# Second layer of a two-layer decoder trunk: residual and block-sum loads queued behind the last pair's T blocks, and the receptance split queued behind the copies of T's lower products

## The chip, the cores and the metric

The kernel runs on one core of one Trainium2 chip. The metric is device time in microseconds (us), lower is better. The engines are named as the profile names them: PE is TensorE's matmul path and PEld its weight loads, DVE is VectorE, ACT is ScalarE, POOL is GpSimd, SP is SyncE, which issues most DMAs here. A letter q behind an engine's name (SPq) means its sequencer, which issues DMAs in order.

## The reference, cut to what matters

`x` has 512 tokens of 2048 channels, all in float32. Layer 0 is gated differential attention, layer 1 is gated RWKV-7 time mixing; each adds its output to `x`. The change lies in layer 1 alone:

```
hn = rms_norm(x);  p = hn @ w_in;  p = p + (shift(p) - p) * mu
r, k, v, g, dw, da = split(p)
decay = exp(-exp(-softplus(-(w0 + tanh(dw) @ decay_up)) - 0.5));  a = sigmoid(a0 + da @ iclr_up)
kk = normalise(k * k_k);  k = k * (1 + (a - 1) * k_a)
per head (32 heads of 64), over the 512 tokens:
    S = S * w_t + (S a_t) b_t^T + v_t k_t^T ;   y_t = S r_t         (a = -kk, b = kk * a)
y = group_norm(y) + sum(r * k * r_k) * v;   x = x + (y * silu(g)) @ w_out
```

## The kernel before

Every large product is made of three passes in a fast float32 format: an operand is split into a high part (rounded by ACT) and a low part (the rest, by DVE), and `mm3` adds high*high, high*low and low*high. The activations of the current layer lie split in `g.hH` and `g.hL`; weights come from memory in 512 KB pieces (`wraw`, three buffers), and `split_w` splits them (`wh` by ACT at L105, `wl` by DVE at L106).

Layer 1 walks over 16 pairs of heads (`for j in range(D // P)` in `layer1`). For a pair it projects k, r, v and the gate with 48 matmuls each (`proj`). The recurrence is done in 8 chunks of 64 tokens. For each chunk a triangular system must be inverted; its inverse is called T. The steps of T that the change and the prediction touch:

- `gram` makes the products `gp` of keys and queries (PE, L1317), copies them to `G` (ACT, L1324) and stores parts of them, with the key norms `ssl` (ACT, L1304), to a scratch `ltd` in memory.
- `t_solve` loads them as `LT` and solves all 32-wide diagonal blocks at once on DVE (`tmpl`, `Tm`, L1376 to L1385); the result goes by DMA to a scratch `td` (L1386).
- `t_combine` loads the blocks from `td` into `TT` by four DMAs (L1405), transposes them on DVE (`T1`, L1415, one instruction for each of the two heads), multiplies on PE (`px<-T,G`, L1421), copies the product to `X` on ACT (L1424), and multiplies again (`px<-TT,X`, L1432) for T's lower block.
- `scan_pair` then goes through the 8 chunks with small matmuls `sm`; it begins with a memset of the first state `VS`.

These steps of one pair, a generator in a `Chain`, are taken in between the next pairs' projections, a step after a given number of matmuls (`tick`). A scheduler with priorities (`high_priority`) then orders each engine's instructions. `with tc.issue_after(ins)` adds one thing to this: what is traced inside it, as far as it is on the engine of `ins`, stands behind `ins` in that engine's order. It adds no wait between engines.

After the 16 pairs comes the output projection: the rows `yd2` are loaded and split (`split_rows`, L461 the loads `yr`), the first two column blocks of `w_out` are multiplied in the plain way (`unit_tok`, for `cb` 0 and 1), and the last two in a scheme with seven products (`seven`), which needs sums of blocks of the rows: `sum_forms` loads the rows again as `frow` (POOL's queue, L677). The old `x` is loaded as `xr` (SP's queue, L1725, 256 KB each, four for each `cb`) and added. All of these loads can be placed by the scheduler as early as their buffers are free: the two `xr` tiles of `cb` 1 take the buffers of `AR` of the pairs 13 and 14.

Beside T, each pair's receptance `r`, shifted and weighted (`mixr`, DVE, L1291), is split by `split_act` (`sHx` on ACT, L1112, `sLx` on DVE), for a sum over channels that `stage_v` takes later.

## Time and profile before

| | |
|---|---|
| time, median of 3 runs | 2075.96 us (2073.53 to 2079.5) |
| the profiled execution's own time | 2081.64 us |
| its span from first to last instruction | 2079.9 us |
| mean granted TensorE clock | 0.997 |
| PE busy | 2055.6 us |
| DVE busy | 1605.1 us |
| ACT busy | 1124.4 us |
| POOL busy | 383.2 us |

The profiled execution took 5.7 us longer than the median of the plain runs, and 1.7 us of its time lie outside the span. Times of rows are us from the span's start. In a row of the timeline stand: start, duration, engine, line, operation, output<-inputs, count, and in brackets the idle time of the engine before it with what ended it. In a row of a table by stages stand: the stage, its length, then for PE, PEld, DVE, ACT and POOL the busy time and the number of instructions, then the granted TensorE clock, the busy share of the 16 DMA engines, and GB/s.

### The profile page before, as it was taken

Reading aid. Unit: us, or ns where it says so; the run is one execution under the profiler, and the core shown is the slowest. Engines: PE = TensorE matmul, PEld = TensorE weight load, DVE = VectorE, ACT = ScalarE, POOL = GpSimd, SP = SyncE. Lnnn points to the kernel's source line nnn. Section 1 sums busy time; section 2 is a strip of 40 time slices with the busy share of each in tenths; the row PEclk is TensorE's granted clock in tenths of the full one; section 3 lists DMA queues with packets and bytes.
Section 4 is the critical chain, followed back from the end, with each engine's and each line's share of the span. In section 5 each row is a group of like instructions: output and inputs, shape, how many; then the busy total and the mean of one; then the engine's idle time right before and its main releaser. Section 6 shows DMA issues by size and latency. Waiting matters only on the chain.

```text
span 2079.9 us, 34162 instructions
## 1 busy us (share of the span) xinstructions
PE 2055.6 (99%) x11948; PEld 1680.2 (81%) x11948; DVE 1605.1 (77%) x4113; ACT 1124.4 (54%) x2238; POOL 383.2 (18%) x765
## 2 busy tenths in 40 slices
PE   9999999999999999999999999999999999999999
PEld 7888888888888888878777778888888888877887
DVE  6988988888888976475778888787777887866645
ACT  5765656565666544345555555555555555545322
POOL 1021211102111000101122322222222222231001
PEclk9999999999999999999999999999999999999999
DMA  8487978879787966823333323323333333345565
GB/s 271 135 178 195 174 176 186 162 196 162 190 176 170 271 214 175 175 80 107 101 82 87 96 77 104 87 86 95 106 92 98 90 95 91 107 136 172 186 163 121
DMA packets 158653, 294.61 MB, mean 142 GB/s; under 512 B 64416, under 2 KB 81824, under 8 KB 158480
## 3 DMA queue, kind: packets, MB, share of 16 engines
q1 hardware_dynamic: 110912, 184.91, 28.8%
q0 software_dynamic: 24928, 87.21, 22.6%
q10 hardware_dynamic: 22640, 20.30, 3.0%
q8 instruction: 94, 1.54, 0.3%
q14 instruction: 79, 0.65, 0.1%
HBM read 268.71 MB, written 23.66 MB: 141 GB/s over the span
## 4 chain that ended last, share of the span: by engine, by line
PE 81%; DVE 11%; DMA 4%; ACT 2%; issue 2%; ACTq 0%; SPq 0%; DVEq 0%; POOLq 0%
PE pp L122 40%; PE pp L573 22%; PE pt L122 5%; DVE wl L106 3%; PE sc L122 1%; PE sm L1509 1%; PE o L122 1%; DMA TT<-td 1%; DMA td<-Tm 1%; PE sm L1527 1%; DVE tmpl L1376 1%; PE gp L1317 1%; PE sm L1520 1%; PE lora L122 1%; PE z L122 1%
## 5 line engine op out<-in xcount | busy, mean ns | idle before, releaser
L106 DVE TENSOR_TENSOR wl<-wraw,wh 128x1024 fp32r<-128x1024 f32 (+2 forms) x291 | 356.1, 1224 | 194.2 <-ACT wh L105 187.7
L105 ACT CAST wh<-wraw 128x1024 fp32r<-128x1024 f32 (+2 forms) x291 | 303.7, 1044 | 269.8 <-PE pp L122 145.4
L122 PE MATMUL pp<-hL,wh 128*128 128x512 f32 x1024 | 414.9, 405 | 0.0
L122 PE MATMUL pp<-hH,wl 128*128 128x512 f32 x1024 | 413.8, 404 | 0.0
L122 PE MATMUL pp<-hH,wh 128*128 128x512 f32 x1024 | 413.6, 404 | 0.0
L122 PEld LDWEIGHTS pp<-hH,wh 128*128 128x128 f32 x1024 | 193.6, 189 | 34.8 <-issue 0.4
L122 PEld LDWEIGHTS pp<-hL,wh 128*128 128x128 f32 x1024 | 193.5, 189 | 33.8
L122 PEld LDWEIGHTS pp<-hH,wl 128*128 128x128 f32 x1024 | 193.7, 189 | 32.4
L573 PE MATMUL pp<-wh,hH 128*128 128x512 f32 x448 | 176.8, 395 | 0.0
L573 PE MATMUL pp<-wh,hL 128*128 128x512 f32 x448 | 175.7, 392 | 0.0
L122 PE MATMUL pp<-wh,hH 128*128 128x512 f32 x372 | 146.5, 395 | 2.0 <-ACT hH L1103 1.8
L122 PE MATMUL pp<-wl,hH 128*128 128x512 f32 x372 | 146.8, 395 | 0.6 <-DVE wl L106 0.5
L122 PE MATMUL pp<-wh,hL 128*128 128x512 f32 x372 | 146.8, 395 | 0.1
L1376 DVE SCALAR_TENSOR_TENSOR tmpl<-LT,Tm 128x60 f32<-128x60 f32 (+24 forms) x496 | 134.2, 270 | 13.3
L573 PE MATMUL pp<-wl,hH 128*128 128x512 f32 x448 | 140.4, 392 | 0.0
L1515 POOL COPY SA<-VS 64x64 f32<-64x64 f32 x224 | 56.7, 253 | 418.3 <-DVE VS L1531 378.2
L1378 DVE TENSOR_TENSOR Tm<-Tm,tmpl 128x60 f32<-128x60 f32 (+24 forms) x496 | 104.1, 210 | 11.7
L1512 ACT COPY rhs<-sm 64x64 f32<-64x64 f32 x256 | 52.8, 206 | 91.2 <-PE sm L1509 88.6
L573 PEld LDWEIGHTS pp<-wl,hH 128*128 128x128 f32 x448 | 84.4, 188 | 17.2
L573 PEld LDWEIGHTS pp<-wh,hH 128*128 128x128 f32 x448 | 84.2, 188 | 17.3 <-issue 0.3
L573 PEld LDWEIGHTS pp<-wh,hL 128*128 128x128 f32 x448 | 84.2, 188 | 16.2
L1522 ACT COPY VS<-sm 64x64 f32<-64x64 f32 x256 | 52.7, 206 | 70.5 <-PE sm L1520 63.9
(402 smaller groups left out, 4376.6 us busy)
## 6 DMA issues: line engine op xcount, KB each, us to landing
wraw<-in_rw_w_in_dram SPq DMA_DIRECT2D x128, 512.0 KB
wraw<-in_da_w_in_dram SPq DMA_DIRECT2D x75, 512.0 KB
wraw<-in_da_w_in_dram POOLq DMA_DIRECT2D x28, 512.0 KB, 6.7
wraw<-in_da_w_out_dram SPq DMA_DIRECT2D x26, 512.0 KB
wraw<-in_rw_w_out_dram SPq DMA_DIRECT2D x26, 512.0 KB
Ta<-in_da_w_in_dram POOLq DMA_DIRECT2D x21, 512.0 KB, 5.7
Tb<-in_da_w_in_dram POOLq DMA_DIRECT2D x21, 512.0 KB, 5.7
Tc<-in_da_w_in_dram POOLq DMA_DIRECT2D x21, 512.0 KB, 5.5
```

Source lines behind the costliest of these rows:

```text
L105: a = nc.scalar.copy(hi[:, ks], raw[:, ks])
L106: d = nc.vector.tensor_sub(lo[:, ks], raw[:, ks], hi[:, ks].bitcast(F32))
L122: m = nc.tensor.matmul(out, a, b, start=s, stop=e, skip_group_check=skip)
L573: m = nc.tensor.matmul(out[t][:], x, wt[lo][:, k, :], start=first, stop=end and lo == 1 and k == KG - 1, skip_group_check=True)
L1317: m = nc.tensor.matmul(gp[h][:, i * P : (i + 1) * P], BK[r_, c0 + i, :, :], p.AR[r_, c0 + i, :, :], start=True, stop=True)
L1376: nc.vector.scalar_tensor_tensor(tt, LT[:, i : i + 1, i + 1 :].to_broadcast([P, s, n]), n2[:, i : i + 1], Tm[:, 0:s, i : i + 1].to_broadca ...
L1378: nc.vector.tensor_add(Tm[:, 0:s, i + 1 :], Tm[:, 0:s, i + 1 :], tt)
L1509: nc.tensor.matmul(sm[:, 0:P], both(p.G[:, c, 0]), both(VS[:, c]), start=True, stop=True)
L1512: nc.scalar.copy(rhs[r_, :], sm[r_, h * C : h * C + C])
L1515: nc.gpsimd.tensor_copy(p.SA[r_, c - 1, :], VS[r_, c, h, :])
L1520: nc.tensor.matmul(sm[:, P : P + C], both(g.TT[j % 2][:, c]), rhs[:], start=True, stop=True)
L1522: g.copied = nc.scalar.copy(VS[r_, c, h, :], sm[r_, P : P + C])
```

## The change

There are three edits, all of the same kind; no instruction is added or taken away.

1. `sum_forms`: the `frow` loads on POOL's queue stand behind the last traced memset of `VS` (`g.begun`).
2. The `xr` loads on SP's queue stand behind the last traced load of T's blocks, `TT<-td` (`g.blocks`). When they are traced, this is that of pair 15, the last one.
3. In the pairs for which `normed` holds, the split of the receptance stands, on ACT, behind the two copies of the product `px` to `X` (`g.lower`).

```diff
@@ sum_forms
-            nc.gpsimd.dma_start(out=r, in_=src[k0 * P : (k0 + KG) * P, :].rearrange(...))
+            with g.tc.issue_after(g.begun):
+                nc.gpsimd.dma_start(out=r, in_=src[k0 * P : (k0 + KG) * P, :].rearrange(...))
@@ t_combine
-            nc.sync.dma_start(
+            g.blocks = nc.sync.dma_start(
                 out=TT[h * C + o : h * C + o + HALF, :, h, o : o + HALF],
-                in_=g.td[j % 2].rearrange(...)[:, l0 : l0 + NC_, :])
+                in_=g.td[j % 2].rearrange(...)[:, l0 : l0 + NC_, :]).ins
...
-        nc.scalar.copy(X[hi], px[hi, :N].rearrange("p (c s) -> p c s", c=NC_))
+        g.lower = nc.scalar.copy(X[hi], px[hi, :N].rearrange("p (c s) -> p c s", c=NC_)).ins
@@ scan_pair
-        nc.gpsimd.memset(VS[r_, 0, h, :], 0.0)
+        g.begun = nc.gpsimd.memset(VS[r_, 0, h, :], 0.0).ins
@@ layer1, behind
-                p.rfs = split_act(g, p.rf[:], w, "x")
+                with tc.issue_after(g.lower) if normed else ExitStack():
+                    p.rfs = split_act(g, p.rf[:], w, "x")
@@ layer1, the first two column blocks
-                nc.sync.dma_start(out=xr[:], in_=g.xd[t * P : (t + 1) * P, cs])
+                with tc.issue_after(g.blocks):
+                    nc.sync.dma_start(out=xr[:], in_=g.xd[t * P : (t + 1) * P, cs])
```

The order of the built programs shows what becomes of this. Line numbers behind the edits are one to three higher in the changed kernel.

ACT's order in one of the pairs, between the cast and shift of the receptance's projection and the copies of `gp`, before:

```order
L105 CAST wh<-wraw 128x1024
L1143 ACTIVATE mixr<-pp,omu 128x512
L1112 CAST sHx<-mixr 128x512
L1304 COPY ssl<-pt 128x128
L1424 COPY X<-px 32x256 x2
L1324 COPY G_14886<-gp 128x8x64 x4
L1435 COPY TT_9513<-px 32x8x32 x2
L105 CAST wh<-wraw 128x1024
```

And the same place now:

```order
L105 CAST wh<-wraw 128x1024
L1144 ACTIVATE mixr<-pp,omu 128x512
L1425 COPY X<-px 32x256 x2
L1305 COPY ssl<-pt 128x128
L1113 CAST sHx<-mixr 128x512
L1325 COPY G_14886<-gp 128x8x64 x4
L1436 COPY TT_9513<-px 32x8x32 x2
L105 CAST wh<-wraw 128x1024
```

`X` and `sHx` have changed places around `ssl`, in the 11 pairs from 5 to 15; the `X` there is that of the pair before.

SP's queue around the store and the load of the last pair's T blocks (`td_80<-Tm_19750`, `TT1_9513<-td_80`), before:

```order
L78 DMA wraw_20259<-in_rw_w_in_dram 128x1024
L78 DMA wraw_20429<-in_rw_w_out_dram 128x1024
L78 DMA TT0_9512<-in_rw_w_out_dram 128x1024
L1725 DMA xr1_21183<-xd_78 128x512 x2
L78 DMA wraw_20481<-in_rw_w_out_dram 128x1024
L1386 DMA td_80<-Tm_19750 128x8x32
L1405 DMA TT1_9513<-td_80 32x8x32 x4
L78 DMA wraw_20538<-in_rw_w_out_dram 128x1024
```

And now:

```order
L78 DMA wraw_20259<-in_rw_w_in_dram 128x1024
L78 DMA wraw_20429<-in_rw_w_out_dram 128x1024
L78 DMA TT0_9512<-in_rw_w_out_dram 128x1024
L78 DMA wraw_20481<-in_rw_w_out_dram 128x1024
L1387 DMA td_80<-Tm_19750 128x8x32
L1406 DMA TT1_9513<-td_80 32x8x32 x4
L78 DMA wraw_20538<-in_rw_w_out_dram 128x1024
```

The two `xr` loads of the second tile are gone from this place; the two of the first tile (`xr1_21176`) have left a place one pair earlier in the same way.

SP's queue further on, where all eight `xr` loads stand now:

```order
L461 DMA yr_20419<-yd2_77 128x512
L1728 DMA xr1_20850<-xd_78 128x512
L1728 DMA xr1_20854<-xd_78 128x512
L1728 DMA xr1_21176<-xd_78 128x512
L78 DMA wraw_20646<-in_rw_w_out_dram 128x1024
L1728 DMA xr1_20858<-xd_78 128x512
L1728 DMA xr1_21176<-xd_78 128x512
L1728 DMA xr1_20862<-xd_78 128x512
L1728 DMA xr1_21183<-xd_78 128x512 x2
L78 DMA wraw_20729<-in_rw_w_out_dram 128x1024
```

The four loads 20850 to 20862, of `cb` 0, stood here before; the four others are new here. On POOL, PE and DVE no row has changed its place: the last pair's memset of `VS` already stood ahead of all `frow` loads.

More of the change, by code (lines that the diff above doesn't have):

```diff
@@ L676, in sum_forms @@
         else:
-            nc.gpsimd.dma_start(out=r, in_=src[k0 * P : (k0 + KG) * P, :].rearrange("(k p) t -> p k t", p=P))
+            with g.tc.issue_after(g.begun):
+                nc.gpsimd.dma_start(out=r, in_=src[k0 * P : (k0 + KG) * P, :].rearrange("(k p) t -> p k t", p=P))
     (a, b), (c, d) = [(r[:, :, 0:256], r[:, :, 256:512]) for r in rows]
@@ L1404, in t_combine @@
             o, l0 = half * HALF, half * 16 + h * NC_
-            nc.sync.dma_start(
+            g.blocks = nc.sync.dma_start(
                 out=TT[h * C + o : h * C + o + HALF, :, h, o : o + HALF],
-                in_=g.td[j % 2].rearrange("q (g l) t -> (q g) l t", g=NG)[:, l0 : l0 + NC_, :])
+                in_=g.td[j % 2].rearrange("q (g l) t -> (q g) l t", g=NG)[:, l0 : l0 + NC_, :]).ins
     T1 = w.tile([P, NC_, HALF], F32, name="T1", tag="T1", bufs=1)
```

## The prediction

> **What bounds the kernel now.** I read the profile's page first, for the share of each engine:

> ```profile
> PE 2055.6 (99%) x11948; PEld 1680.2 (81%) x11948; DVE 1605.1 (77%) x4113; ACT 1124.4 (54%) x2238; POOL 383.2 (18%) x765
> ```

> PE is busy for 99% of the span, so a new order on other engines can give back only what PE loses: 24.3 us of idle time (2079.9 - 2055.6), and time in which it runs at a lower clock. Next the waits of PE, longest in total first (us in total, times, longest):

> ```profile
> PE px L1421 <- DVE T L1415: 4.1, 2, 3.3
> PE sm L1509 <- DVE VS L1531: 2.9, 8, 0.9
> PE px L1432 <- ACT X L1424: 2.7, 4, 0.7
> ```

> The first and the third lie where the change works. The first is one place, the last pair's T; the third is four equal waits in four pairs. The second is the recurrence itself, which the change leaves alone.

> For the third I read the timeline of PE and of ACT in one of the four pairs:

> ```profile
> 1417.33 2.06 PE L1317 MATMUL gp<-AR,BK 64*128 64x128 f32 x32
> 1420.06 0.69 PE L1432 MATMUL px<-TT,X 32*32 32x32 f32 x32 [0.68 <-ACT X L1424]
> ```

> ```profile
> 1418.46 0.62 ACT L1112 CAST sHx<-mixr 128x512 fp32r<-128x512 f32 x1 [4.65 <-DVE mixr L1291]
> 1418.98 0.26 ACT L1304 COPY ssl<-pt 128x128 f32<-128x128 f32 x1
> 1419.26 0.74 ACT L1424 COPY X<-px 32x256 f32<-32x256 f32 x2
> 1420.03 2.06 ACT L1324 COPY G<-gp 128x512 f32<-128x512 f32 x4
> ```

> ACT has been idle for 4.65 us when it takes up `sHx`, because `sHx` waits for DVE's `mixr`; `X` stands behind it. What `X` reads, `px<-T,G`, stands ahead of `gp` in PE's order and so was done by 1417.33. PE ends `gp` at 1419.39 and then waits 0.68 us for `X`.

> For the first I read the queues of SP and POOL around the last pair's T, and DVE, ACT and PE behind it:

> ```profile
> 1872.34 0.80 SPq L1725 DMA_DIRECT2D xr<-xd  x2
> 1875.53 0.33 SPq L78 DMA_DIRECT2D wraw<-in_rw_w_out_dram  x1
> 1877.71 0.37 SPq L1386 DMA_DIRECT2D td<-Tm  x1
> 1886.06 1.80 SPq L1405 DMA_DIRECT2D TT<-td  x4
> ...
> 1900.53 0.33 SPq L78 DMA_DIRECT2D wraw<-in_rw_w_out_dram  x1
> ```

> ```profile
> 1872.10 1.51 POOL L677 DMA_DIRECT2D frow<-yd  x2 [4.01 <-PE Y L1553]
> 1877.99 0.72 POOL L677 DMA_DIRECT2D frow<-yd  x1 [4.37 <-DVE Tm L1385]
> 1879.32 0.57 POOL L1483 DMA_DIRECT2D yd<-mixv  x1 [0.61 <-DVE rs_i L65]
> ```

> ```profile
> 1887.84 0.44 DVE L1415 STREAM_TRANSPOSE T<-TT 64x256 f32<-64x256 f32 x1 [4.46 <-DMA TT<-td]
> 1888.21 0.70 DVE L1144 SCALAR_TENSOR_TENSOR mixv<-pp,mu,mixv 128x511 f32<-128x511 f32 x1
> 1888.84 0.15 DVE L71 SCALAR_TENSOR_TENSOR rs_i<-rs_t,rs_i 128x8 f32<-128x8 f32 x1
> 1888.91 0.68 DVE L452 TENSOR_TENSOR hL<-yr,hH 128x512 fp32r<-128x512 f32 x1
> 1889.62 0.44 DVE L1415 STREAM_TRANSPOSE T<-TT 64x256 f32<-64x256 f32 x1
> ```

> ```profile
> 1888.34 0.31 PE L1421 MATMUL px<-T,G 32*32 32x32 f32 x2 [3.31 <-DVE T L1415]
> 1888.58 0.80 PE L122 MATMUL pp<-hH,wh 128*128 128x512 f32 x1
> 1890.12 1.06 PE L1421 MATMUL px<-T,G 32*32 32x32 f32 x30 [0.74 <-DVE T L1415]
> ```

> The store `td` is issued at 1877.71, and the loads `TT`, which wait for its landing, at 1886.06: 8.35 us. One pair earlier the same step takes 2.74 us:

> ```profile
> 1819.86 0.37 SPq L1386 DMA_DIRECT2D td<-Tm  x1
> 1822.60 1.85 SPq L1405 DMA_DIRECT2D TT<-td  x4
> ```

> The last pair's store stands in SP's queue behind 0.52 MB of `xr` (two loads of 256 KB, as the code has them) and 0.52 MB of `wraw`, while POOL's queue moves `frow`. PE has nothing else in its order, and stands still from 1885.03 (1888.34 less 3.31). The table by stages shows what this costs besides (the last three figures: clock, DMA share, GB/s):

> ```profile
> 1872.00:1875.00 3.00, 3.00 (x19) 2.46 (x14) 2.90 (x12) 1.05 (x1) 1.51 (x2) 1.00 0.57 107
> ...
> 1877.70:1880.00 2.30, 2.30 (x12) 1.91 (x11) 2.23 (x7) 1.95 (x3) 1.30 (x2) 1.00 1.00 382
> ...
> 1888.30:1891.70 3.40, 2.62 (x35) 1.89 (x36) 3.34 (x7) 1.64 (x5) 0.00 (x0) 0.50 0.86 242
> 1891.70:1895.10 3.40, 3.40 (x9) 2.31 (x7) 3.40 (x8) 2.62 (x5) 0.00 (x0) 0.50 0.97 292
> ```

> After the stall PE runs at half its clock for two stages of 3.40 us. Of its 6.02 busy us there (2.62 + 3.40), half is lost, 3.0 us. With the idle 4.05 us (3.31 + 0.74) the last pair's T costs 7.05 us now.

> **The change, part by part.** The loads of the block sums: nothing, since no row of POOL's queue moves. No chance is spent on it.

> The split of the receptance, in 11 pairs. In the four that wait, ACT can copy `X` while it idles: from 1417.33 at the latest to 1418.07 (0.74), then `ssl` to 1418.33 (0.26), then `sHx` at 1418.46 as before, since `mixr` sets it, and `G` from 1419.08. `X` is there 1.3 us before PE wants it, so the wait is gone: 4 x 0.68 = 2.7 us. Next in line is nothing on this path; `G` comes sooner. In the other seven pairs `sHx` is ready sooner, and it and `G` may now slip behind `X` and `ssl`, by up to 1.0 us (0.74 + 0.26). In the four waiting pairs `G` starts as late as 2.70 us behind the start of `gp` (1420.03 - 1417.33), and the list of waits shows nothing on PE that came of it; I take nothing for this. Bounds: 0 to 2.7 us gained.

> The residual loads. The first pair of `xr` loads also leaves SP's queue, one pair before, where PE does not wait for T; no gain. The second pair leaves the place ahead of `td`. How much sooner does `td` land? If all engines are shared and busy, 0.52 MB at 382 GB/s is 1.4 us; if the store falls back to what the pair before shows, 5.6 us (8.35 - 2.74). I take a value between: SP's queue shares the engines with POOL's, and at half of 382 GB/s the `xr` loads hold it for 2.7 us. Then the first transpose starts at 1885.1 instead of 1887.84 and ends at 1885.6.

> What is late next is the second transpose. In DVE's order it stands behind `mixv`, which needs ACT's part, which waits for the landing of another transfer:

> ```profile
> 1885.67 0.69 ACT L1143 ACTIVATE mixv<-pp,omu 128x512 f32<-128x512 f32 x1 [3.38 <-DMA yd<-mixv]
> ...
> 1919.22 1.05 ACT L105 CAST wh<-wraw 128x1024 fp32r<-128x1024 f32 x1 [1.42 <-PE pp L122]
> ```

> `yd<-mixv` goes through POOL's queue behind `frow`. With 0.52 MB less to move I let it land 1.4 us sooner, so ACT starts at 1884.3 and ends at 1885.0. DVE then needs 0.70 + 0.15 + 0.68 us to 1886.5, and 0.44 us for the transpose: 1887.0. PE, which stops at 1885.03, waits 0.5 us for the first product and 1.1 us for the rest: 1.6 us instead of 4.05.

> Does the clock still fall? The trace has one more such place, at its start:

> ```profile
> 17.80:21.20 3.40, 1.58 (x6) 0.75 (x5) 1.12 (x1) 2.19 (x3) 0.00 (x0) 1.00 0.98 348
> 21.20:24.60 3.40, 3.27 (x8) 2.38 (x8) 1.75 (x4) 1.52 (x3) 0.00 (x0) 0.50 1.01 380
> ```

> There a stage with 1.82 us of idle time (3.40 - 1.58) is followed by one at half clock, which costs half of 3.27, 1.6 us. My 1.6 us of idle time in two pieces lie just below that, so I count no half clock, and keep 1.6 us for the range. [...]

> The part gains 7.05 - 1.6 = 5.45 us; bounds 1.4 us (a later landing, and the clock falls as before) to 7.05 us.

> The loads that are held now follow `yr`, with 1.05 MB more to move beside the weights. The piece issued at 1900.53 is cast at 1919.22, 18.7 us later. At 382 GB/s the 1.05 MB cost 2.7 us of these; I count nothing.

> **Sum:** 2.7 + 5.45 = 8.15 us. The profiled execution took 2081.64 us (span 2079.9), so it would take 2073.5. The median of the plain runs is 5.7 us below it; I take the same gain off 2075.96: **2067.8 us**. No change that is smaller than 0.3% (6.2 us) can be told from none here.

> **The rivals.**

> *The store still lags.* `td` lands only 1.4 us sooner; PE still idles 2.65 us and loses 3.0 us to the clock. Gain 1.4 + 2.7 = 4.1: 2071.9 us. For it: `frow` stays where it was, and the rate was only 107 GB/s at 1872 with `xr` alone starting. Against it: the 2.74 us of the pair before. Chance 0.2. [...]

> *The plain runs stall less than the profiled one.* They are 2.1 to 8.1 us shorter; if the median run never fell to half clock there, its gain lacks 3.0 us: 8.15 - 3.0 = 5.15, 2070.8 us. Chance 0.15.

> *The four waits move on.* `px<-TT,X` is ready at once, but PE waits as long for `rhs` or `gp`, as ACT's and DVE's later rows have not moved. Only 5.45 us are gained: 2070.5 us. Against it: ACT's rows behind `X` come sooner in these pairs. Chance 0.1.

> *The held loads starve the output projection: slower.* They stand in SP's queue ahead of weights. It decides once a piece lands more than 18.7 us behind its issue. At 107 GB/s, the lowest rate quoted, 1.05 MB of `xr` and 0.52 MB of the piece take 14.7 us, so it needs another 4 us. If PE then stood still twice, each time at this stage's price of 7.05 us, the sum would be 14.1 - 8.15 = 6 us slower: 2082 us. Chance 0.05.

> **How the numbers follow.** The forecast has 0.5. Plain runs scatter by about 3 us around their median, so a gain of 8.15 us shows as more than 6.2 us in 0.8 of the cases, 4.1 us in 0.25, 5.15 us in 0.35, 5.45 us in 0.4. Faster: 0.5 x 0.8 + 0.2 x 0.25 + 0.15 x 0.35 + 0.1 x 0.4 = 0.54. Slower: 0.05. The same: 0.41. The range goes from the most that the bounds give (7.05 + 2.7 = 9.75, 2066.2 us) less 3 us of scatter, 2063, to the lagging store with 2 us of scatter, 2074.

> **What would show it.** In the profile of the changed kernel the wait of `px<-TT,X` for `X` is gone from PE's list, and `X` starts before `sHx` in the pairs. Between the last `td` and `TT` lie some 5.6 us or less instead of 8.35. PE's wait for the last transposes is near 1.6 us in sum, and no stage behind it shows a clock of 0.50. I am wrong if `td` still takes 7 us or more, if the clock falls as before, if PE shows new waits in the pairs for `gp` or `rhs`, or if `wh` casts behind 1900 wait for `wraw`.

## The result and the profile after

The changed kernel takes **2069.46 us** in the median (2068.74 to 2072.04, 7 runs) against 2075.96 us before (2073.53 to 2079.5, 7 runs): ratio 0.9969, 95% interval 0.9958 to 0.9981, 6.5 us less. In two more sessions (the experiments both_again and both_third below) it was 7.1 and 5.2 us less. Its profiled execution took 2070.32 us (span 2068.6), 11.3 us less than that of before. The page, the busy time of each engine:

```profile
PE 2051.0 (99%) x11948; PEld 1680.1 (81%) x11948; DVE 1605.3 (78%) x4113; ACT 1122.7 (54%) x2238; POOL 383.2 (19%) x765
```

The waits of PE (us in total, times, longest). Every line of the code stands one to three later than before:

```profile
PE sm L1510 <- DVE VS L1532: 2.9, 8, 0.9
...
PE px L1422 <- DVE T L1416: 0.6, 1, 0.6
```

The wait for `X` has left the list, the wait for T fell from 4.1 to 0.6 us, and the recurrence's own wait is as it was. The pair that answers to the one at 1417 before, first ACT, then PE:

```profile
1414.51 0.74 ACT L1425 COPY X<-px 32x256 f32<-32x256 f32 x2 [3.20 <-PE px L1422]
1415.27 0.27 ACT L1305 COPY ssl<-pt 128x128 f32<-128x128 f32 x1
1415.43 0.62 ACT L1113 CAST sHx<-mixr 128x512 fp32r<-128x512 f32 x1
1415.95 2.05 ACT L1325 COPY G<-gp 128x512 f32<-128x512 f32 x4
```

```profile
1414.72 2.06 PE L1318 MATMUL gp<-AR,BK 64*128 64x128 f32 x32
1416.70 0.47 PE L1433 MATMUL px<-TT,X 32*32 32x32 f32 x18
```

`X` now stands ahead of `ssl` and `sHx`; it ends at 1415.25, 1.45 us before PE takes it up, and no bracket stands behind PE's row.

The queues of SP and POOL around the last pair's T, then DVE and PE behind it:

```profile
1872.72 0.38 SPq L1387 DMA_DIRECT2D td<-Tm  x1
1877.21 1.81 SPq L1406 DMA_DIRECT2D TT<-td  x4
...
1886.29 2.06 SPq L1728 DMA_DIRECT2D xr<-xd  x3
```

```profile
1874.27 0.57 POOL L1484 DMA_DIRECT2D yd<-mixv  x1 [0.60 <-DVE rs_i L65]
...
1878.32 0.69 ACT L1144 ACTIVATE mixv<-pp,omu 128x512 f32<-128x512 f32 x1 [1.07 <-DMA yd<-mixv]
```

```profile
1878.95 0.44 DVE L1416 STREAM_TRANSPOSE T<-TT 64x256 f32<-64x256 f32 x1 [0.60 <-DMA TT<-td]
...
1884.37 0.69 DVE L1582 TENSOR_TENSOR yc<-yc,rsg 128x512 f32<-128x512 f32 x1
```

```profile
1879.91 0.24 PE L1422 MATMUL px<-T,G 32*32 32x32 f32 x2
...
1881.22 0.69 PE L1422 MATMUL px<-T,G 32*32 32x32 f32 x30 [0.63 <-DVE T L1416]
...
1885.53 0.60 PE L1589 MATMUL pt<-ident,yc 128*128 128x128 f32 x4
```

From `td` to `TT` it is 4.49 us now (8.35 before), from `yd`'s issue to ACT's `mixv` 4.05 (1885.67 - 1879.32 = 6.35 before). The stages behind it (clock, DMA share and GB/s at the end):

```profile
1880.00:1883.40 3.40, 2.77 (x40) 2.11 (x41) 3.34 (x9) 3.34 (x7) 0.00 (x0) 1.00 0.96 288
1883.40:1886.80 3.40, 3.40 (x47) 2.66 (x46) 3.40 (x7) 2.51 (x6) 0.00 (x0) 1.00 0.97 299
```

No stage has the clock of 0.50 that before had twice here.

**Where the 11.3 us lie.** The first and the last `gp` from the sixth pair on, before and after:

```profile
1239.30 2.06 PE L1317 MATMUL gp<-AR,BK 64*128 64x128 f32 x32
1832.62 2.06 PE L1317 MATMUL gp<-AR,BK 64*128 64x128 f32 x32
```

```profile
1237.76 2.06 PE L1318 MATMUL gp<-AR,BK 64*128 64x128 f32 x32
1827.59 2.06 PE L1318 MATMUL gp<-AR,BK 64*128 64x128 f32 x32
```

These ten pair steps took 593.32 us and take 589.83: **3.49 us** less. From the last `gp` to the end of the span, which I call the tail, it was 247.28 us and is 241.01: **6.27 us** less. The other 1.54 us lie ahead of the sixth pair, nearly all in the first layer, where no instruction moved; that part is chance. To split the tail, two rows of before are wanted:

```profile
1893.27 0.68 DVE L1581 TENSOR_TENSOR yc<-yc,rsg 128x512 f32<-128x512 f32 x1
```

```profile
1896.63 0.60 PE L1588 MATMUL pt<-ident,yc 128*128 128x128 f32 x4
```

Counted from the last `gp`, the first transpose starts at 51.36 us instead of 55.22: 3.86 us sooner. DVE then needs the same time to `yc` (5.42 and 5.43 us). PE takes up `yc` 1.16 us behind its start instead of 3.36: 2.20 us less, and from there to the end 0.20 us remain. So the later T cost 3.86 us, which DVE passed on, and the half clock 2.20 us, by which PE fell behind DVE. The same 2.20 us come out of PE alone: its order of matmuls is the same in both kernels, and from its second product behind T to `pt<-ident,yc`, a stretch in which it waits for nothing, it needs 6.51 us before (1890.12 to 1896.63) and 4.31 after (1881.22 to 1885.53).

### The profile page after: what moved, and what is told of

The parts are those of the page before. It is cut to its first block, busy times and chain, and to the rows that moved or that the text cites. A ratio compares the mean times of both kernels' runs of the same rounds, so it can differ in the third digit from the quotient of the medians.

```text
span 2068.6 us, 34162 instructions
## 1 busy us (share of the span) xinstructions
PE 2051.0 (99%) x11948; PEld 1680.1 (81%) x11948; DVE 1605.3 (78%) x4113; ACT 1122.7 (54%) x2238; POOL 383.2 (19%) x765
## 3 DMA queue, kind: packets, MB, share of 16 engines
q8 instruction: 94, 1.54, 0.3%
## 4 chain that ended last, share of the span: by engine, by line
PE 86%; DVE 9%; ACT 2%; DMA 1%; issue 1%; ACTq 0%; SPq 0%; DVEq 0%; POOLq 0%
PE pp L122 43%; PE pp L573 22%; PE pt L122 5%; DVE wl L106 2%; PE sm L1510 2%; PE gp L1318 1%; PE sc L122 1%; PE o L122 1%; PE sm L1528 1%; PE sm L1521 1%; PE lora L122 1%; PE z L122 1%; DVE tmpl L1377 1%; DMA pair<-in_xT_dram 1%; PE Y L1550 1%
## 5 line engine op out<-in xcount | busy, mean ns | idle before, releaser
L105 ACT CAST wh<-wraw 128x1024 fp32r<-128x1024 f32 (+2 forms) x291 | 303.6, 1043 | 271.7 <-PE pp L122 135.3
L122 PE MATMUL pp<-hL,wh 128*128 128x512 f32 x1024 | 414.6, 405 | 0.0
L122 PE MATMUL pp<-hH,wl 128*128 128x512 f32 x1024 | 413.5, 404 | 0.0
L122 PE MATMUL pp<-hH,wh 128*128 128x512 f32 x1024 | 413.2, 403 | 0.0
L122 PEld LDWEIGHTS pp<-hH,wh 128*128 128x128 f32 x1024 | 193.3, 189 | 34.5 <-issue 0.4
L122 PEld LDWEIGHTS pp<-hL,wh 128*128 128x128 f32 x1024 | 193.3, 189 | 33.6
L122 PEld LDWEIGHTS pp<-hH,wl 128*128 128x128 f32 x1024 | 193.5, 189 | 32.3
L122 PE MATMUL pp<-wh,hH 128*128 128x512 f32 x372 | 146.8, 395 | 1.7 <-ACT hH L1104 1.7
L122 PE MATMUL pp<-wh,hL 128*128 128x512 f32 x372 | 147.0, 395 | 0.1
L122 PE MATMUL pp<-wl,hH 128*128 128x512 f32 x372 | 146.5, 394 | 0.5 <-DVE wl L106 0.5
```

The lines of the kernel that those rows point to most:

```text
L105: a = nc.scalar.copy(hi[:, ks], raw[:, ks])
L122: m = nc.tensor.matmul(out, a, b, start=s, stop=e, skip_group_check=skip)
```

## The experiments

Four sessions on four chips; the kernel before ran beside them, with medians of 2080.06 us (33 runs), 2078.81 (31), 2078.04 (17) and 2078.43 (17). Each kernel is compared within its session. Since one execution of a kernel differs from the next, the medians and the profiles are read apart. The last two columns are of the profile alone.

| kernel | session | median us | against before us | ratio, 95% interval | ten pair steps us | tail us |
|---|---|---|---|---|---|---|
| only_split | 1 | 2075.98 | -4.1 | 0.9984, 0.9975 to 0.9992 | 589.94 | 246.1 |
| only_residual | 1 | 2074.34 | -5.7 | 0.9975, 0.9965 to 0.9984 | 594.35 | 240.6 |
| only_sums | 1 | 2077.51 | -2.6 | 0.9988, 0.9978 to 0.9999 | 592.86 | 246.2 |
| one_ahead | 1 | 2075.62 | -4.4 | 0.9983, 0.9974 to 0.9993 | 590.14 | 244.7 |
| both_again | 2 | 2071.72 | -7.1 | 0.9972, 0.9963 to 0.9980 | 590.15 | 240.7 |
| residual_again | 2 | 2073.98 | -4.8 | 0.9982, 0.9973 to 0.9991 | 593.12 | 240.5 |
| kept_busy | 2 | 2076.92 | -1.9 | 0.9997, 0.9987 to 1.0007 | 592.70 | 244.9 |
| sums_behind | 2 | 2070.62 | -8.2 | 0.9966, 0.9953 to 0.9978 | 589.84 | 240.7 |
| kept_full | 3 | 2081.84 | +3.8 | 1.0021, 1.0009 to 1.0032 | 595.97 | 246.6 |
| first_free | 4 | 2071.69 | -6.7 | 0.9969, 0.9957 to 0.9982 | 589.76 | 240.8 |
| sums_again | 4 | 2071.41 | -7.0 | 0.9964, 0.9952 to 0.9976 | 589.92 | 240.8 |
| both_third | 4 | 2073.23 | -5.2 | 0.9974, 0.9965 to 0.9983 | 590.97 | 241.3 |

**Each edit alone.** only_split has edit 3, only_residual edit 2, only_sums edit 1 of the change, as the diff shows them.

```
only_split:     g.lower = nc.scalar.copy(X[hi], ...).ins
                with tc.issue_after(g.lower) if normed else ExitStack():
                    p.rfs = split_act(g, p.rf[:], w, "x")
only_residual:  g.blocks = nc.sync.dma_start(out=TT[...], ...).ins
                with tc.issue_after(g.blocks):
                    nc.sync.dma_start(out=xr[:], ...)
only_sums:      g.begun = nc.gpsimd.memset(VS[...], 0.0).ins
                with g.tc.issue_after(g.begun):
                    nc.gpsimd.dma_start(out=r, ...)
```

> Edit 3 alone: the receptance split stands behind the copies of px to X in 11 pairs, all loads stand as before. Theory A, the two edits act at two separate places and add up: the four waits of px<-TT,X for X (0.68 us each) are gone and the pairs step at 58.99 us each, 3.5 us gained from pair 5 to pair 15, while PE still stands about 4 us before the last pair's T, with td to TT near 8 us and two stages at half clock behind it; plain runs about 3.4 us faster, ratio 0.998. Rival B, the four waits show only in the profiled execution and the plain runs owe all of their 6.5 us to the loads: the ratio of the plain runs is 1.000. Rival C, the earlier pairs carry over into the last stage: td to TT falls below 6 us here too.

> Edit 2 alone: the xr loads stand behind the last pair's TT loads, ACT's order is as before. Theory A: td to TT takes 4 to 5 us instead of 8.35, PE waits under 1.5 us for the last transposes and keeps its full clock, the waits of px<-TT,X for X stay at some 2 to 3 us in all; profiled execution about 6 us shorter than before's; plain runs about 3 us faster (what is left of 6.5 us after 3.4 us for the split), ratio 0.9985. Rival B: the plain runs gain the whole 6.5 us here, ratio 0.997. Rival C: td is late whatever stands ahead of it, td to TT stays above 7 us and nothing is gained.

> Edit 1 alone: the frow loads behind the memset of VS. No row of any queue or engine moves, so this is the program of before once more. Both theories: ratio 1.000 within 0.1%. It is run for the states of its single executions: if the half clock behind the last pair's T comes and goes from one execution to the next, the mean clocks of its runs show two values (0.997 and 0.999), and the times differ by some 5 us with them; its profiled execution then may show td to TT well under 8 us. If the half clock always comes, all runs show 0.997.

In the profiles the two places come apart cleanly. only_split has the pair steps of the whole change (589.94 us) and the stall of before. PE's two waits for T in it, and its windows around them:

```profile
1884.22 0.24 PE L1421 MATMUL px<-T,G 32*32 32x32 f32 x2 [2.71 <-DVE T L1415]
...
1886.00 0.69 PE L1421 MATMUL px<-T,G 32*32 32x32 f32 x30 [1.11 <-DVE T L1415]
```

```profile
1879.86:1883.27 3.41, 1.66 (x8) 1.04 (x6) 0.03 (x1) 0.97 (x2) 0.00 (x0) 1.00 0.10 26
1883.27:1886.68 3.41, 1.35 (x34) 0.95 (x34) 2.88 (x6) 2.73 (x5) 0.00 (x0) 1.00 0.70 155
1886.68:1890.09 3.41, 3.41 (x9) 2.73 (x9) 3.41 (x9) 3.10 (x6) 0.00 (x0) 0.50 0.99 309
```

only_residual has no wait for T at all, no half clock, the tail of the whole change, and three of the waits for `X`, whose row in PE's list is:

```profile
PE px L1432 <- ACT X L1424: 2.0, 3, 0.7
```

only_sums has before's order of instructions on every engine and queue, and yet its median is 2.6 us below before's, and its interval leaves out the 1.000 that was expected. That is what chance can do in a session, so an interval that misses 1.000 by as little proves nothing here. So the medians of the single edits (4.1 and 5.7 us) must not be added up, and alone they don't decide between theory A and rival B: only_residual's 5.7 us lie nearer to B's 6.5 than to A's 3, while only_split isn't at B's 1.000 but hardly below only_sums. What speaks for A are the profiles, and the next session's direct comparison.

**How much must stand ahead of the store?** In one_ahead all three edits are kept, but one `xr` load of 256 KB may go ahead of the last `td` again.

```
-                with tc.issue_after(g.blocks):
+                with tc.issue_after(g.blocks) if (cb, t) in ((0, 0), (0, 1), (0, 2), (0, 3), (1, 3)) else ExitStack():
```

> All edits, but the first xr tile's two loads stand one pair earlier as before, and one of the second tile's two loads (256 KB) stands ahead of td as before, the other behind TT. A dose between before (two loads ahead of td) and the changed kernel (none). If the loads in SP's queue are what holds td, td to TT lies between 4.5 and 8.35 us, near 6.4, and PE's wait for the last transposes between 0.6 and 4.05 us, near 2 us; the half clock may or may not come. If only the full queue matters, it is as with none ahead: 4.5 us and 0.6 us. Plain runs: 1 to 3 us slower than the changed kernel.

SP's queue in it:

```profile
1869.13 0.33 SPq L1728 DMA_DIRECT2D xr<-xd  x1
1872.33 0.33 SPq L78 DMA_DIRECT2D wraw<-in_rw_w_out_dram  x1
1874.51 0.38 SPq L1387 DMA_DIRECT2D td<-Tm  x1
1881.09 1.81 SPq L1406 DMA_DIRECT2D TT<-td  x4
```

The store takes 6.58 us to `TT`, between 8.35 and 4.49, although the `xr` load is issued 5.4 us ahead of it; PE waits 2.69 us, a window of half clock follows, and the tail is 3.7 us longer than in the changed kernel, with none ahead. In the tail, one load gives back more than half of what holding two had won. The step scatters from one execution to the next, though: with two `xr` loads ahead it took 6.04 us (kept_full), 6.40 (kept_busy), 7.73 (only_split), 8.01 (only_sums) and 8.35 (before), with none 3.27 to 4.75. Two against none is shown; one against two is one profile.

What the end of the slow step is, the stages of before just ahead of `TT` show (DMA share and GB/s at the end):

```profile
1884.00:1885.00 1.00, 1.00 (x5) 0.53 (x3) 0.00 (x0) 0.00 (x0) 0.00 (x0) 1.00 0.07 25
1885.00:1886.00 1.00, 0.03 (x1) 0.00 (x0) 0.00 (x0) 0.33 (x1) 0.00 (x0) 1.00 0.04 6
```

A share of 0.07 of 16 engines is the work of about one (0.07 x 16 = 1.1): nearly all transfers had ended, and `TT`, issued at 1886.06, waited for what one engine still had to do. The trace's DMA packets show what that was. From about 1883.7 to 1885.05, packets of 4096 bytes from POOL's queue and of 128 bytes from the store take turns, one of each in about 0.17 us. So in the last 2 of the 8.35 us the step waits for one late engine. Holding the `xr` loads shortened the step with `frow` still on POOL's queue. Whether moving `frow` alone would have done so, or whether the `xr` loads would do the same harm from another queue, is not shown.

**The whole change beside one edit.** both_again is the changed kernel; residual_again is only_residual.

> The whole change, unchanged, on this chip beside the three below. Theory A (two separate places, added up; single edits gave 4.1 us for the split and 5.7 us for the residual loads): 8 to 10 us below the kernel before in the median; the profile again with a pair step of 58.97 to 58.99 us in every pair from the fifth on and 241.0 us from the last gp to the end. Theory B (the edits share a part of their gain): 6.5 us or less, though the profile shows both stalls gone.

> The residual loads alone. Theory A: 4.5 to 6 us below the kernel before, and the whole change another 2.7 to 3.9 us below this one (four or five pairs at 0.68 to 0.87 us). Theory B: the whole change no more than 1.5 us below this one.

On one chip the whole change is 2.26 us below the residual loads alone (ratio of the means 0.9988, 0.9983 to 0.9993): the split counts in plain runs too, with less than the 2.97 us of the two profiles' pair steps (593.12 - 590.15). The 2.26 us lie between what theory A (2.7 or more) and theory B (1.5 or less) named, and so do the 7.1 us of the total (8 or more, 6.5 or less).

**Is the half clock a cost of its own?** kept_busy is before with six useless matmuls in PE's order at the place of the wait, kept_full with eighteen (`9 * (0, 1)`). In the rows each of them counts as two.

```
+    if j == D // P - 1:
+        for c in 3 * (0, 1):
+            both = p.G[:, c, 0].rearrange("p h n -> p (h n)")
+            nc.tensor.matmul(px[:, 0:P], both, both, start=True, stop=True)
```

> The kernel before, with six matmuls of G with itself ahead of the last pair's px, into a part of px that the next products overwrite; they fill about 2.5 us of the 4 us in which PE waits for T, and T comes no sooner. Theory G (the half clock behind the stall is a cost of its own): no clock of 0.50 behind the last pair; from the last gp to the end 243.8 to 245.6 us instead of 246.2 to 247.3 (one or two windows of 3.41 us at half clock are 1.7 or 3.4 us), so 1.7 to 3 us below the kernel before. Theory H (in these windows other engines set the pace, and the clock costs nothing): the half clock goes too, but the tail stays at 246 us or more and the time within 0.5 us of before.

> The kernel before with eighteen matmuls of G with itself in the place where kept_busy has six: kept_busy showed 0.25 us for each, so they take 4.5 us and outlast both waits for T (4.1 us in before), from which no useful work is gained. Theory G (the half clock is a cost of its own): no clock of 0.50 behind the last pair, px starts 56.9 us after the last gp, and from there to the end it takes 187.4 us as in the changed kernel, instead of 191 to 191.6 us; the tail is 244.3 us, below the 246.2 to 247.3 of the kernels with the stall, although PE does 4.5 us of useless work. Theory H (other engines set the pace there): no half clock either, but 190 us or more from px to the end, and a tail of 247 us or more.

kept_busy decides little: six matmuls took only 1.50 us, one wait of 1.82 us stayed, and the clock fell for one window. Its tail of 244.9 us lies in theory G's range, but T came sooner in this execution too (6.40 us from `td` to `TT`), and the insert moved `pt<-ident,yc` ahead of three `pp` matmuls. In kept_full the clock stays up behind the last pair, but another wait appears. PE in kept_full, and its windows there:

```profile
1887.38 4.18 PE L1422 MATMUL px<-G 128*128 128x128 f32 x36
1891.49 0.69 PE L1425 MATMUL px<-T,G 32*32 32x32 f32 x32
1894.38 0.63 PE L1592 MATMUL pt<-ident,yc 128*128 128x128 f32 x4 [2.19 <-DVE yc L1585]
```

```profile
1889.51:1892.92 3.41, 2.68 (x51) 2.44 (x49) 3.35 (x8) 1.07 (x3) 0.00 (x0) 1.00 0.92 306
1892.92:1896.33 3.41, 1.95 (x11) 1.72 (x12) 3.41 (x8) 3.01 (x6) 0.00 (x0) 1.00 0.96 310
1896.33:1899.74 3.41, 3.41 (x45) 2.63 (x44) 2.87 (x5) 3.06 (x6) 0.00 (x0) 1.00 0.88 309
```

PE, no longer slowed, stands still 2.19 us for DVE's `yc`, and the tail is 246.6 us: not the 244.3 that theory G named, nor H's 247 or more. From `px` to the end it takes 190.2 us (2081.7 - 1891.49), which H named and G didn't. DVE is late because T is late. But the long insert moved `pt<-ident,yc` ahead of `px<-TT,X` and a dozen `pp` matmuls, and moved some casts of ACT and DVE, so a part of the wait, and of the 3.8 us by which it is slower in the median, can come of the new order. It does not settle the clock's price by itself. (Its ten pair steps are long because of a chance stall near 1537, far ahead of the edit.) What bears the 2.20 us above are traces in which PE's order is the same. PE's second product, `yc` on DVE, and `yc` on PE in only_sums:

```profile
1887.27 1.06 PE L1422 MATMUL px<-T,G 32*32 32x32 f32 x30 [1.10 <-DVE T L1416]
```

```profile
1890.42 0.69 DVE L1582 TENSOR_TENSOR yc<-yc,rsg 128x512 f32<-128x512 f32 x1
```

```profile
1893.06 0.60 PE L1589 MATMUL pt<-ident,yc 128*128 128x128 f32 x4
```

PE takes `yc` up 3.36 us behind its start with two windows of half clock (before), 2.64 with one (only_sums), 1.16 with none (after); from the second product to there PE needs 6.51, 5.79 and 4.31 us.

**What is left of the wait.** sums_behind sends the `frow` loads through SP's queue behind the T blocks, which edit 1 leaves on POOL's queue where they were; sums_again is the same kernel. first_free lets the first `xr` tile (two loads, one pair earlier) go as before. both_third is the changed kernel.

```
sums_behind:  -  with g.tc.issue_after(g.begun):
              -      nc.gpsimd.dma_start(out=r, ...)
              +  with g.tc.issue_after(g.blocks):
              +      nc.sync.dma_start(out=r, ...)
first_free:   -  with tc.issue_after(g.blocks):
              +  with tc.issue_after(g.blocks) if not cb or t > 1 else ExitStack():
```

> The whole change, and the loads of the block sums (frow) really moved: they go through SP's queue behind the T blocks, where in the changed kernel they stay on POOL's. If frow is what still keeps td and yd in the last pair: td to TT falls from 4.49 to about 3 us, yd to ACT's mixv from 4.05 to about 3 us, the last 0.63 us of PE's wait for T goes, and the time falls by 0.6 us, too little to tell. If wraw, which stays ahead of td, keeps it: td to TT stays above 4 us. If the sums are wanted early: a new wait behind them, and the time rises.

> The whole change, but the first tile of xr (two loads, one pair earlier, where nothing waits) is not held. If only what stands ahead of the last td counts: the profile's tail and pair steps as with the whole change (240.7 to 241.0 us, 58.97 to 58.99), no wait for T above 0.7 us, and the time within 1 us of it. If holding the first tile brings something too, or costs something later (six instead of eight loads behind the blocks): a tail that differs by more than 0.5 us.

> sums_behind again, beside the whole change on one chip: in the first session it was 1.1 us below the whole change, less than the spread of either. If the 0.6 us wait and the closer T are worth something in most executions: again 0.6 to 1.5 us below. If not: within 0.5 us, or above.

> The whole change a third time, as the measure for the two above: 6.5 to 8 us below the kernel before, as in the two sessions so far (6.5 and 7.1).

In sums_behind `td` to `TT` takes 2.85 us, close to the 2.74 of one pair earlier:

```profile
1873.27 0.38 SPq L1387 DMA_DIRECT2D td<-Tm  x1
1876.12 1.85 SPq L1406 DMA_DIRECT2D TT<-td  x4
```

But in sums_again it is 3.90 us, and in the three executions of the whole change 4.49, 3.27 and 4.75; so, once the `xr` loads are held, `frow` is at most a part of what is left. sums_behind is 1.1 us below the whole change on its chip (ratio of the means 0.9997, 0.9992 to 1.0002), sums_again 1.8 us below (0.9992, 0.9987 to 0.9997). It has the lowest ratio to before of all, but first_free, with nothing new ahead of T, was 1.5 us below the same runs of the whole change (0.9995, 0.9989 to 1.0001; within 1 us was expected). Those runs, both_third, won 5.2 us where 6.5 to 8 were expected. I don't take the gain over the changed kernel as shown. That first_free is no slower, with the same steps and tail, shows no worth in holding the first tile.

## Why the prediction was right, step by step

**The split.** Right in mechanism. The wait is gone, `X` is 1.45 us ahead of PE (predicted 1.3), and no other wait took its place; the rival that the waits move on is ruled out by only_split. The term was too small: 4 x 0.68 us is the idle time alone. A pair that waited took 59.8 us from `gp` to `gp` and one that didn't 58.97, 0.8 us apart, and a fifth pair lost 0.3 us more. 3.49 us in the profile instead of 2.7.

**The loads.** Right in place and in kind. The term's parts were off on the same side. T came 3.86 us sooner, not 2.7; `yd` 2.3, not 1.4; the rest of PE's waits is 0.63 us, not 1.6. The value taken between the bounds shared all engines by rate and left 5.6 us from `td` to `TT`; with no `xr` load ahead the step took 3.27 to 4.75 us. The 2 us in which before waited for one late engine, which no rate tells of, are gone too: in after the DMA share is still 0.86 from 1875.0 to 1877.2, when `TT` is issued. For the clock I took half of all that PE did in the two stages, 3.0 us; it came to 2.20. Of the 6.02 us of work, about 1.0 lie ahead of the second wait for T, where a faster PE would only have waited longer; of the other 4.99 (1890.12 to 1895.11) half is 2.5 us, near the 2.20. Together 6.27 us instead of 5.45. The rival of the lagging store is out in the profile of the changed kernel, although before had a late engine (the packets from 1883.7 to 1885.05); one_ahead, with one of the two loads held, comes near it (6.58 us to `TT`, 2.69 us of waits, the clock down).

**No half clock** was right. The guess that 1.6 us of idle time is just too little (1.82 us at before's start were followed by half clock) wasn't tried by the changed kernel, which kept 0.63.

**Held loads, output projection.** From `pt<-ident,yc` to the end the kernel takes 183.07 us instead of 183.27; nothing starves.

**The sum, and the step that failed.** The two places together won 3.49 + 6.27 = 9.8 us in the profile, more than the 8.15 of the sum; the median won 6.5. The step that failed is the last one: "I take the same gain off 2075.96". That a plain run stalls less than the profiled one, which I gave 0.15, is what the medians point to. So the forecast of 2067.8 us came within 1.7 us of 2069.46 in part by luck: terms that were 1.6 us too small stood against a transfer to the median that was 3.3 us too generous (9.8 - 6.5). The profiled execution of before was a costly one of its kind: two windows of half clock behind a stall of 4.05 us. only_sums, with the same order, shows one such window, a tail 1.0 us shorter and pair steps 0.5 us shorter. Over the four sessions, the 98 runs of before sort by their mean granted clock like this, beside the 22 of both_again and both_third:

| granted clock | runs of before | mean us | runs of the whole change | mean us |
|---|---|---|---|---|
| 0.996 | 4 | 2082.5 | 0 | |
| 0.997 | 22 | 2080.5 | 1 | 2076.8 |
| 0.998 | 46 | 2079.0 | 5 | 2073.8 |
| 0.999 | 18 | 2076.5 | 10 | 2072.5 |
| 1.000 | 8 | 2074.6 | 6 | 2071.1 |

A window of 3.41 us at half clock loses 1.7 us of the full clock (an estimate, half of 3.41), 0.0008 of the run, so a row stands for about one window more or less, wherever it lies in the run; before's own profile, with a mean of 0.997, has one at the start too (from 21.2), where nothing was changed. At the same clock the change wins 3.5 to 5.2 us; the rest of its gain is that most runs have moved up a row. A quarter of before's runs (26 of 98) stand at 0.999 or above and had less to win. This accounts for the direction. It doesn't account for all: against only_sums' profile, the mean of the three profiles of the whole change (590.3 and 241.0 us) still wins 2.5 + 5.2 = 7.7 us, 0.6 to 2.5 us more than the three medians. The plain runs leave no trace, so what they stall is open.

## What to carry to other kernels

A small store on whose landing a chain waits was worth more than its size here: loads of 256 KB that nobody needs for a long time, issued 5 us ahead on the same queue, made it take 6.0 to 8.4 us instead of 3.3 to 4.8. Hold such loads behind the store. A price from another place bounds the gain and no more: the pair before, with its 2.74 us, also had a piece of `wraw` and a `yr` load ahead of its store, but no `frow` on POOL's queue:

```profile
1816.35 0.33 SPq L78 DMA_DIRECT2D wraw<-in_rw_w_in_dram  x1
1817.04 0.32 SPq L461 DMA_DIRECT2D yr<-yd  x1
```

So what stands ahead has to be read with what other queues move at the time, and with how far the step ends behind the bulk of the transfers. When a profiled execution runs longer than the median, size each term also by the better executions, before taking its gain off the median.

## What the runs showed of the hardware

```profile
1884.07:1887.48 3.41, 1.52 (x39) 1.22 (x38) 2.76 (x6) 3.15 (x6) 0.00 (x0) 1.00 0.67 144
1887.48:1890.89 3.41, 3.41 (x20) 2.67 (x15) 3.41 (x9) 3.34 (x8) 0.00 (x0) 0.50 0.95 290
```

With 1.35 us (only_split's second row, with two pauses) it fell too, and with 1.58 at before's start; with 1.66 (only_split's first row) and 1.95 (kept_full, a 2.19 us pause cut in two by a window's border, with the windows counted on from the half clock at that trace's start) it stayed. That is not a limit at a busy time between 1.58 and 1.66 us, as the start of only_split shows:

```profile
16.18:19.59 3.41, 2.10 (x10) 1.40 (x8) 0.18 (x1) 1.25 (x2) 0.00 (x0) 1.00 0.83 226
19.59:23.00 3.41, 2.47 (x6) 1.09 (x7) 2.46 (x3) 1.14 (x2) 0.00 (x0) 1.00 1.03 400
23.00:26.41 3.41, 3.41 (x9) 2.62 (x9) 1.50 (x2) 2.28 (x3) 0.00 (x0) 0.50 1.04 402
```

There 2.47 us of busy time, in six matmuls that stand apart, were followed by half clock. So the profile's busy time of a window tells only roughly whether the clock will fall (behind 1.66 us it stayed, behind 2.47 us it fell), and the limit stays open. In before the clock stayed low for a second window, after one with 0.80 us of idle time:

```profile
1888.28:1891.69 3.41, 2.61 (x34) 1.89 (x35) 3.35 (x7) 1.65 (x5) 0.00 (x0) 0.50 0.85 240
1891.69:1895.11 3.42, 3.42 (x9) 2.31 (x7) 3.42 (x8) 2.63 (x5) 0.00 (x0) 0.50 0.97 292
```

So in before two pauses of PE, 3.31 and 0.74 us, of which neither fills a window of 3.41 us, were followed by two windows of half clock.
